# A transformer block on one core: where four of seven kept sums wait, when two columns of x are made, and two products in plain fp32

## The chip, the core and the metric

The kernel runs on one core of a Trainium2 chip. The core has five engines with instruction streams of their own: TensorE (PE, matrix products; its weight loads are shown as PEld), VectorE (DVE), ScalarE (ACT), GpSimd (POOL) and SyncE (SP). They meet at semaphores. SP's queue issues the loads, POOL's the transfers that add into their destination. The metric is the time of one launch on the device in microseconds (us), lower is better. The time before is 1423.77 us, the median of three runs (1421.55 to 1423.99).

## The reference

One decoder layer over 256 tokens of width 2048, in fp32: attention and a short gated convolution, merged by sigmoid gates; then a squared-ReLU MLP of width 8192, and a gated embedding. Cut to what matters here, the MLP and what follows it:

```python
h = rms_norm(r, g_mlp[i])
r = r + jnp.square(jax.nn.relu(h @ w_up[i])) @ w_down[i]
h = rms_norm(r, g_ple[i])
r = r + jax.nn.sigmoid(h @ w_ple_gate[i]) * (p[i] @ w_ple_proj[i])
```

## The kernel before

**Products.** A product in fp32 is made of three in fp32r: the operands are split into a high part (a copy on ACT, `high`) and a low part (a subtraction on DVE, `low`), and PE adds high·high, high·low and low·high. A product can also be left in plain fp32, without the split; PE then takes more time for it, and the kernel calls such pairs NATIVE (line 687): before, only the last pair, and of it only T1 and T3.

**The up/down stage** (lines 963 to 1066) runs over 72 units `g`: 64 columns of w_up, then 8 of w_down. A unit's column product (`cols`, ps_up or ps_dn) is followed on PE by the seven products P1 to P7 of one *pair* of the down product, which is done by a scheme of Strassen and Winograd: 7 products of 2x2 blocks in place of 8. A pair is (side, j); its blocks of w_down come as four loads into a `raw_s` tile (`load_pair`), and `make` forms B11, B22, B21 and the sums T1 to T4 from them; S1 to S4 are sums of the activations. T1 and T3 of three pairs in eight (ADDED, line 688) are not added by DVE: the blocks are loaded into a tile with the tag `t` (two rooms, `load_added`), and a DMA of POOL adds the other blocks to it (line 706). The seven products stay in PSUM banks from pair to pair.

**The two sides.** Side 0 and side 1 take the banks in turns. When a side ends, the seven sums go out (`store`): ACT evacuates a bank to a `part` tile, and a DMA of POOL adds it to a room in device memory. Side 0 comes back for good at pair (0, 20), in unit 51 to 52 (`resumed`): then its seven kept sums, loaded back in unit 46 (`fetch_kept`, RESUME), are copied into the banks (`resume`, on ACT for P1, P5, P2 and P4, on DVE for the others), each right behind the evacuation of the other side's sum from that bank. These steps stand in the list `filling` and are let in one by one between the work of `make` and of the next unit.

**Rooms and order.** `part`, the kept sums, x and many others come from one pool of 44 slots; a tile that finds no free slot waits until one is released, and the instruction that writes it waits with all that stands behind it on its engine. From unit 2 on every engine keeps the program's order (`inorder`), and so does SP's queue: a load that waits for a room holds those behind it.

**The end of the stage.** In units 69 to 71, x for the gate's products is entered from the finished columns of r (`enter_high` on ACT, `enter_low` on DVE): 8 and 9, then 10 to 12, then 13 and 14. In unit 71, p1 (P1 scaled, on ACT), d, e and f begin the four blocks c11, c12, c21 and c22 of the down product. PE goes on with `half_gate(0, 1)` over columns 8 to 15, and then transposes c11 and c21 (`turn`).

Of the kernel before, what the change touches and what calls it, by code (L numbers as in the profile page):

```python
# [8 lines left out]
F32 = mybir.dt.float32  # L9
# [9 lines left out]
P = 128  # L19
# [5 lines left out]
CW = 512  # L25
# [13 lines left out]
def hybrid_block_kernel(ctx: ExitStack, tc: tile.TileContext, ins: dict, out: bass.AP):  # L39
# [12 lines left out]
    wp = ctx.enter_context(tc.tile_pool(name="wp", bufs=N_PART))  # L52
# [5 lines left out]
    def slot(shape, dtype, name):  # L58
        return bp.tile(shape, dtype, tag="slot", name=name)
# [35 lines left out]
    def load(*args):  # L95
        dma = nc.sync.dma_start(*args)
        return tc.keep_in_program_order(dma) if ordered[0] or ordered_loads[0] else dma
# [37 lines left out]
    def high(hi, src):  # L135
        act(hi, src, AF.Copy)
# [417 lines left out]
    for c in range(4):  # L554
        gates = []
        for i in range(2):
            ps = rows(tiles("w_in", 24 + 16 * i + 4 * c), xT, f"g{i}_{c}", pops=2)
            g = [slot([P, CW], F32, f"g{i}_{c}_{t}") for t in range(NT)]
# [54 lines left out]
    N_GROUP, GROUP = 6, 4  # L613
    N_BOTH = N_GROUP * GROUP
    hP = {}
    uT, u_raw, wS, sums, wU, evac = {}, {}, {}, {}, {}, {}
# [4 lines left out]
    NU = len(units)  # L621
# [4 lines left out]
    items = []  # L626
# [14 lines left out]
    g = FIRST  # L641
# [32 lines left out]
    def half_tiles(name):  # L674
        return tuple(wp.tile([P, HALF], F32R, tag=t, name=f"{name}_{t}") for t in ("hi", "lo"))
# [9 lines left out]

    LAST = len(items) - 8
    NATIVE = {items[-1]}
    ADDED = {items[n] for n in range(GROUP, LAST) if (n - GROUP) % (2 * GROUP) in (0, 4, 6)} | set(items[LAST:])

    def pair_part(a, n, d):  # L690
        side, j = a
        n += 16 * (j // 8) + 8 * side
        k = 2 * (j % 8) + d
        return ins["w_down"][n:n + 4, :, k * P:(k + 1) * P].rearrange("n p m -> p n m")
# [3 lines left out]
    def load_pair(a):  # L698
# [3 lines left out]
        for i, block in enumerate(BLOCKS):  # L702
            if i != 2 or a not in ADDED:
                load(raw[:, i, :].rearrange("p (n m) -> p n m", n=4), pair_part(a, *block))
        if a in ADDED:
            nc.gpsimd.dma_start(wS[a]["t13"], raw[:, 0:2, :], accum_op=ALU.add)  # L706

    def load_added(a):

        wS[a] = {}  # L710
        if a in ADDED:
            t = wS[a]["t13"] = wp.tile([P, 2, CW], F32, tag="t", name="t13", bufs=2)
# [3 lines left out]
    def sum_u(j):  # L716

        a11, a12, a21, a22 = (u_raw[2 * j + k][:, t * P:(t + 1) * P] for t in range(2) for k in range(2))
        s = slot([P, 4, P], F32, "s_raw")
        dve.tensor_sub(s[:, 0, :], a21, a22)  # L720
        dve.tensor_sub(s[:, 2, :], s[:, 0, :], a11)
        dve.tensor_sub(s[:, 1, :], a11, a21)
        dve.tensor_add(s[:, 3, :], a12, s[:, 2, :])
        return s
# [13 lines left out]
    def make(a, xs, evacuate, work):  # L738


        w, j = wS[a], a[1]
        raw = w["raw"]
        flat, halves = "p a f -> p (a f)", "p (a f) -> p a f"
        fresh = None
        if 0 in xs:
            if j not in sums:
                fresh = sum_u(j)
                sums[j] = tuple(slot([P, 4, P], F32R, f"s_{i}") for i in range(2))
            sh, sl = sums[j]
            for i, name in enumerate(("S1", "S3", "S2", "S4")):  # L750
                w[name] = sh[:, i, :], sl[:, i, :]
            if a in NATIVE:
                w["S1"], w["S3"] = fresh[:, 0, :], fresh[:, 1, :]
                fresh, sh, sl = (t[:, 2:, :] for t in (fresh, sh, sl))
            hi, lo = half_tiles("b")
            keep(w, ("B11", "B22"), hi, lo)
            src = raw[:, 0:2, :].rearrange(flat)
            high(hi, src)
            evacuate()
            if fresh is not None:  # L760
                high(sh, fresh)
            low(lo, src, hi)
            if a in ADDED:
                t13 = w["t13"]
            else:
                t13 = raw[:, 0:3:2, :]
                dve.tensor_add(t13, raw[:, 0:2, :], raw[:, 2:3, :].to_broadcast([P, 2, CW]))
            w["raw13"] = t13
        if 2 in xs:
            b21 = w["B21"] = tuple(slot([P, CW], F32R, f"b21_{n}") for n in range(2))  # L770
            high(b21[0], raw[:, 3, :])
            evacuate()
            fill()
            dve.tensor_add(raw[:, 1, :], raw[:, 1, :], w["raw13"][:, 0, :])
            if 0 in xs:
                low(b21[1], raw[:, 3, :], b21[0])
                dve.tensor_add(raw[:, 3, :], raw[:, 1, :], raw[:, 3, :])
                raw24 = raw[:, 1:4:2, :]
            else:
                dve.tensor_add(raw[:, 2, :], raw[:, 1, :], raw[:, 3, :])  # L780
                low(b21[1], raw[:, 3, :], b21[0])
                raw24 = raw[:, 1:3, :]
                work()
        if 0 in xs:
            if fresh is not None:
                low(sl, fresh, sh)
            if 2 not in xs:
                work()
            if a in NATIVE:
                w["T1"], w["T3"] = w["raw13"][:, 0, :], w["raw13"][:, 1, :]  # L790
                fill()
            else:
                t13 = half_tiles("t13")
                keep(w, ("T1", "T3"), *t13)
                view = [t.rearrange(halves, a=2) for t in t13]
                high(view[0], w["raw13"])
                fill()
                low(view[1], w["raw13"], view[0])
        if 2 in xs:
            t24 = half_tiles("t24")  # L800
            keep(w, ("T2", "T4"), *t24)
            view = [t.rearrange(halves, a=2) for t in t24]
            high(view[0], raw24)
            fill()
            low(view[1], raw24, view[0])
# [6 lines left out]
    NAMES = ("P1", "P3", "P5", "P7", "P2", "P6", "P4")  # L812

    def products(a, x):
        j = a[1]
        for name, left, b, n0, n1 in PRODUCTS[x]:
            if a in first_of and a != resumed and n0 == 0:
                prod[name] = pp.tile([P, CW], F32, tag=f"b{int(name[1]) - 1}", name=name)
            if left[0] == "A":
                at = slice((int(left[1]) - 1) * P, int(left[1]) * P)  # L820
                k = 2 * j + int(left[2]) - 1
                xs = [uT[k][:, h, at] if k in uT else first_half(k)[:, h, :] for h in range(2)]
            else:
                xs = wS[a][left]
            if a in NATIVE and b in ("T1", "T3"):
                if n0 == 0:
                    mm(prod[name], xs, wS[a][b], start=False, skip_group_check=True, stop=a in last_of or a == items[-1])
                continue
            for n in range(n0, n1):
                mm(prod[name], xs[n == 2], wS[a][b][n == 1], start=a in first_of and a != resumed and n == 0, skip_group_check=a in items[resumed_at:], stop=(a in last_of or a == items[-1]) and n == 2)  # L830
# [12 lines left out]
    def scaled(dst, src, by, other, how=ALU.add):  # L843
        dve.scalar_tensor_tensor(dst, src, by, other, op0=ALU.mult, op1=how)
# [3 lines left out]
    resumed = [a for a in items if a in first_of][-1]  # L848
    resumed_at = items.index(resumed)

    def fetch_kept():
        kept = {}
        for name in NAMES:
            kept[name] = slot([P, CW], F32, "part_in")
            load(kept[name], parts[0, name])
        return kept

    def resume(name, st):
        prod[name] = pp.tile([P, CW], F32, tag=f"b{int(name[1]) - 1}", name=name)
# [26 lines left out]
    def fill(n=1):  # L886
        for _ in range(min(n + (n == 1 and len(filling) > 7), len(filling))):
            filling.pop(0)()
# [32 lines left out]
    def enter_high(n):  # L921
        hP[n] = slot([P, 2, S], F32R, "x")
        act(hP[n][:, 0, :], r[n // 2][:, n % 2, :], AF.Copy, scale=col(G_PLE + n))

    def enter_low(n):
        x = hP[n]
        dve.scalar_tensor_tensor(x[:, 1, :], r[n // 2][:, n % 2, :], col(G_PLE + n), x[:, 0, :].bitcast(F32), op0=ALU.mult, op1=ALU.subtract)
# [25 lines left out]
    RESUME, SUMS = 46, (56, 59)  # L953
# [9 lines left out]
    for g in range(NU):  # L963
        kind, i = units[g]
# [10 lines left out]
            if x == 0:  # L975
                load_added(a)
        if g == RESUME:
            kept = fetch_kept()
        if g in SUMS:
            sum_part(SUMS.index(g))  # L980
        for u in {NU - 8: (4, 5, 6, 7), NU - 4: (0, 1), NU - 3: (2, 3)}.get(g, ()):
# [6 lines left out]
        xs = hT if kind == "up" else {k: uT[16 * i[0] + k] for k in range(16)}  # L988
# [56 lines left out]
        if g == NU - 1:  # L1045
            p1 = [evacuated(prod["P1"], "p1", by) for by in (up0, up1)]
            d, e = (slot([P, CW], F32, n) for n in "de")
            scaled(d, prod["P5"], up0, p1[0], ALU.subtract)
            scaled(e, prod["P3"], up0, d)
            f = slot([P, CW], F32, "f")  # L1050
            scaled(f, prod["P7"], up1, p1[1])
        entering = {NU - 3: (8, 9), NU - 2: (10, 11, 12), NU - 1: (13, 14)}.get(g, ())
        for n in entering:
            enter_high(n)
            if n % 2 == 1:
# [198 lines left out]
```

## Time and profile before

| | |
|---|---|
| median of three timed runs | 1423.77 us |
| the profiled execution | 1418.83 us |
| its span | 1416.9 us |
| granted TensorE clock | 0.999 |
| ACT busy | 880.3 us (62%) |
| DVE busy | 1103.2 us (78%) |
| POOL busy | 202.3 us (14%) |
| HBM, read and written | 294.43 and 22.54 MB |

A row of a timeline shows the start and the length in us, the engine, line, operation, and what is written and read, with partitions x elements; a bracket gives the idle time of the engine just before it, and what ended that. "x3" means three instructions merged. Nearly every PE, ACT and DVE row has the line of a helper (90, 87, 101), so the tiles tell them apart. Buffer numbers are left out: P is any of the seven sums, t_hi the high part of T1/T3 or of T2/T4, t a tile of the two rooms. A row of the view of waits gives the time in all, the number of times and the longest. A row of the view of windows gives, for a stretch, its length, the busy time of PE, PEld, DVE, ACT and POOL, and then the granted clock, the share of the DMA engines and GB/s. In the view of DMA issues the last number is the time from issue to landing.

### The profile page before, as it was taken

The numbers are of one execution on the slowest core, as the hardware profiler recorded it, in microseconds if no ns is written. First come the engines' busy times: TensorE is split into PE (matmuls) and PEld (weight loads), VectorE is DVE, ScalarE is ACT, GpSimd is POOL, SyncE is SP. The second block draws the span as 40 slices with busy tenths as digits, with TensorE's granted clock in tenths as the row PEclk, the third lists the DMA queues.
The fourth block names the chain that finished last, engine by engine and source line by source line (L and its number), as shares of the span: only waits on it lengthen the run. The fifth ranks groups of instructions, "written<-read, shape, count | busy, mean of one in ns | idle before, by whom it ended". The sixth has DMA issues, their size and how long they took to land.

```text
span 1416.9 us, 19839 instructions
## 1 busy us (share of the span) xinstructions
PE 1406.4 (99%) x7023; PEld 1192.1 (84%) x7023; DVE 1103.2 (78%) x1676; ACT 880.3 (62%) x1433; POOL 202.3 (14%) x311
## 2 busy tenths in 40 slices
PE   9999999999999999999999999999999999999998
PEld 7888888888888888888888888888888878888888
DVE  7666666766555656665999999999998989888984
ACT  6765545554535444445777777778786767655752
POOL 0034464311120200000010100101010010110000
PEclk9999999999999999999999999999999999999999
DMA  9868787775666675663788888989899799998470
GB/s 290 305 218 261 221 245 231 234 224 198 219 202 213 210 266 191 211 223 95 225 279 248 266 244 238 276 257 256 259 233 318 236 237 271 272 284 268 154 255 23
DMA packets 220547, 331.39 MB, mean 234 GB/s; under 512 B 13600, under 2 KB 145184, under 8 KB 206368
## 3 DMA queue, kind: packets, MB, share of 16 engines
q1 hardware_dynamic: 201936, 287.08, 62.3%
q0 software_dynamic: 18368, 43.01, 13.2%
q8 instruction: 55, 0.90, 0.3%
q14 instruction: 44, 0.36, 0.1%
q10 hardware_dynamic: 144, 0.04, 0.0%
HBM read 294.43 MB, written 22.54 MB: 224 GB/s over the span
## 4 chain that ended last, share of the span: by engine, by line
PE 86%; DMA 5%; DVE 4%; issue 2%; ACT 2%; SPq 0%; POOL 0%; DVEq 0%; POOLq 0%; ACTq 0%
PE ps_up L90 20%; PE P L90 14%; PE ps_g L90 12%; PE ps_o L90 7%; PE ps_pg L90 6%; PE ps_y L90 6%; PE ps_q L90 3%; PE ps_cx L90 3%; PE ps_k L90 3%; PE ps_cb L90 3%; PE ps_cc L90 3%; PE ps_v L90 3%; DMA raw_s<-in_w_down_dram 2%; DVE w_lo L101 1%; DMA t<-in_w_down_dram 1%
## 5 line engine op out<-in xcount | busy, mean ns | idle before, releaser
L101 DVE TENSOR_TENSOR w_lo<-raw,w_hi 128x512 fp32r<-128x512 f32 (+1 forms) x524 | 467.9, 926 | 187.3 <-ACT w_hi L87 161.9
L87 ACT ACTIVATE w_hi<-raw 128x512 fp32r<-128x512 f32 (+1 forms) x524 | 407.0, 815 | 258.9 <-PE ps_g L90 63.1
L90 PE MATMUL ps_up<-x,w_hi 128*128 128x512 f32 x1024 | 253.4, 390 | 0.0
L90 PEld LDWEIGHTS ps_up<-x,w_hi 128*128 128x128 f32 x1024 | 192.0, 188 | 37.8 <-ACT up L87 0.6
L90 PE MATMUL ps_g<-w_hi,x 128*128 128x512 f32 x512 | 158.2, 389 | 0.0
L87 ACT ACTIVATE t_hi<-raw_s 128x1024 fp32r<-128x1024 f32 x88 | 93.5, 1062 | 94.3 <-DVE raw_s L101 94.2
L90 PEld LDWEIGHTS ps_up<-x,w_lo 128*128 128x128 f32 x1024 | 131.3, 191 | 5.0
L90 PE MATMUL ps_up<-x,w_lo 128*128 128x256 f32 x1024 | 132.8, 283 | 0.0
L90 PE MATMUL P<-t_hi,s 128*128 128x512 f32 x332 | 121.3, 392 | 2.6 <-ACT P L87 1.4
L90 PEld LDWEIGHTS ps_g<-w_hi,x 128*128 128x128 f32 x512 | 96.1, 188 | 19.9
L101 DVE TENSOR_TENSOR t_lo<-raw_s,t_hi 128x1024 fp32r<-128x1024 f32 x88 | 106.3, 1220 | 4.8 <-ACT t_hi L87 4.8
L101 DVE TENSOR_TENSOR raw_s<-raw_s 128x512 f32<-128x512 f32 (+1 forms) x120 | 100.1, 834 | 4.1
L90 PE MATMUL ps_g<-w_lo,x 128*128 128x512 f32 x256 | 99.6, 389 | 0.0
L706 POOL DMA_DIRECT2D t<-raw_s x24 | 20.5, 853 | 479.8 <-DVE b_lo L101 122.5
L90 PE MATMUL ps_y<-w_hi,x 128*128 128x512 f32 x256 | 79.4, 389 | 0.0
L90 PEld LDWEIGHTS P<-t_hi,s 128*128 128x128 f32 x332 | 62.6, 189 | 16.7 <-ACT P L87 2.5
L101 DVE TENSOR_TENSOR b_lo<-raw_s,b_hi 128x1024 fp32r<-128x1024 f32 x56 | 68.2, 1218 | 4.0 <-ACT b_hi L87 4.0
L90 PE MATMUL ps_pg<-x,w_hi 128*128 128x512 f32 (+1 forms) x272 | 67.9, 380 | 1.0 <-DVE x L101 1.0
L87 ACT ACTIVATE up<-ps_up 128x512 f32<-128x512 f32 x64 | 37.7, 590 | 45.3 <-PE ps_up L90 45.2
L90 PE MATMUL P<-t_lo,s 128*128 128x512 f32 x166 | 64.9, 391 | 0.0
L87 ACT ACTIVATE a<-a 128x256 f32<-128x256 f32 x128 | 53.2, 415 | 11.3 <-DVE a L101 9.5
L87 ACT ACTIVATE b_hi<-raw_s 128x1024 fp32r<-128x1024 f32 x56 | 58.8, 1050 | 0.0
(239 smaller groups left out, 2547.3 us busy)
## 6 DMA issues: line engine op xcount, KB each, us to landing
raw<-in_w_up_dram SPq DMA_DIRECT2D x64, 1024.0 KB, 7.3
raw<-in_w_in_dram SPq DMA_DIRECT2D x56, 1024.0 KB, 5.4
raw_s<-in_w_down_dram SPq DMA_DIRECT2D x200, 256.0 KB, 4.5
raw<-in_w_branch_dram SPq DMA_DIRECT2D x16, 1024.0 KB, 5.7
raw<-in_w_o_dram SPq DMA_DIRECT2D x16, 1024.0 KB, 4.9
raw_first<-in_w_qkv_dram SPq DMA_DIRECT2D x48, 256.0 KB, 6.4
raw<-in_w_qkv_dram SPq DMA_DIRECT2D x12, 1024.0 KB, 6.8
t<-in_w_down_dram SPq DMA_DIRECT2D x48, 256.0 KB, 5.9
```

What stands on the lines that cost most here:

```text
L87: return inorder(nc.scalar.activation(*args, **kw))
L90: return inorder(nc.tensor.matmul(*args, **kw))
L101: return lambda *args, **kw: inorder(getattr(nc.vector, name)(*args, **kw))
L706: nc.gpsimd.dma_start(wS[a]["t13"], raw[:, 0:2, :], accum_op=ALU.add)
```

## The change

Four things. The kept sums are fetched in three lots: P5, P7 and P2 in slots in unit 46; P1 and P3 in one `t` room in unit 47; P6 and P4 in one in unit 49. The pair that would have used that room, (0, 20), is no longer ADDED, so DVE adds its T1 and T3. Column 13 of x is entered in unit 70 with 10 to 12, and column 14 between p1, d and e in unit 71. And the last pair's T2 and T4 are left in plain fp32, as T1 and T3 were, with S2 and A22 unsplit.

```diff
-    ADDED = {items[n] for n in range(GROUP, LAST) if (n - GROUP) % (2 * GROUP) in (0, 4, 6)} | set(items[LAST:])
+    ADDED = {items[n] for n in range(GROUP, LAST) if (n - GROUP) % (2 * GROUP) in (0, 4, 6)} - {items[LAST - GROUP]} | set(items[LAST:])
...
             if a in NATIVE:
-                w["S1"], w["S3"] = fresh[:, 0, :], fresh[:, 1, :]
-                fresh, sh, sl = (t[:, 2:, :] for t in (fresh, sh, sl))
+                for i, name in enumerate(("S1", "S3", "S2")):
+                    w[name] = fresh[:, i, :]
+                w["A22"] = u_raw[2 * j + 1][:, P:]
+                fresh, sh, sl = (t[:, 3:, :] for t in (fresh, sh, sl))
...
-        if 2 in xs:
+        if 2 in xs and a in NATIVE:
+            w["T2"], w["T4"] = raw24[:, 0, :], raw24[:, 1, :]
+            fill()
+        elif 2 in xs:
             t24 = half_tiles("t24")
...
-            if left[0] == "A":
+            if left in wS[a]:
+                xs = wS[a][left]
+            else:
                 at = slice((int(left[1]) - 1) * P, int(left[1]) * P)
                 k = 2 * j + int(left[2]) - 1
                 xs = [uT[k][:, h, at] if k in uT else first_half(k)[:, h, :] for h in range(2)]
-            else:
-                xs = wS[a][left]
-            if a in NATIVE and b in ("T1", "T3"):
+            if a in NATIVE and b[0] == "T":
...
-    def fetch_kept():
-        kept = {}
-        for name in NAMES:
-            kept[name] = slot([P, CW], F32, "part_in")
+    kept = {}
+
+    def fetch_kept(names, pair=False):
+        if pair:
+            room = wp.tile([P, 2, CW], F32, tag="t", name="kept", bufs=2)
+        for i, name in enumerate(names):
+            kept[name] = room[:, i, :] if pair else slot([P, CW], F32, "kept")
             load(kept[name], parts[0, name])
-        return kept
...
         if g == RESUME:
-            kept = fetch_kept()
+            fetch_kept(NAMES[2:5])
+        if g == RESUME + 1:
+            fetch_kept(NAMES[:2], pair=True)
+        if g == RESUME + 3:
+            fetch_kept(NAMES[5:], pair=True)
...
             d, e = (slot([P, CW], F32, n) for n in "de")
+            enter_high(14)
             scaled(d, prod["P5"], up0, p1[0], ALU.subtract)
+            enter_low(14)
             scaled(e, prod["P3"], up0, d)
...
-        entering = {NU - 3: (8, 9), NU - 2: (10, 11, 12), NU - 1: (13, 14)}.get(g, ())
+        entering = {NU - 3: (8, 9), NU - 2: (10, 11, 12, 13)}.get(g, ())
```

`NAMES` is P1, P3, P5, P7, P2, P6, P4. Three places of the instruction streams show what moves.

ACT in unit 51 and 52, from the first evacuation of the ending side on. P1 to P4 are the banks, `part` the evacuated sums, part_in and kept the kept ones, t13_hi and t24_hi the high parts of T1/T3 and T2/T4. In brackets stands what an instruction waits for: PE, DVE, ACT itself, a DMA of SP (DMAHW) or of POOL (DMASW). Before:

```order
L87 ACTIVATE part_10677<-P1_9926 128x512 [waits PE_49]
L87 ACTIVATE P1_10680<-part_in_10061 128x512 [waits Activation_49]
L87 ACTIVATE t13_hi_10685<-t13_10385 128x1024 [waits DMAHW1_49,DMAHW0_49,DMASW0_49]
L87 ACTIVATE part_10688<-P3_9930 128x512 [waits DMASW4_49,Activation_49]
L87 ACTIVATE t24_hi_10694<-raw_s_10488 128x1024 [waits DVE_49]
L87 ACTIVATE part_10697<-P5_9934 128x512 [waits DMASW1_49]
L87 ACTIVATE P5_10700<-part_in_10065 128x512 [waits Activation_49]
L87 ACTIVATE w_hi_10745<-raw_10592 128x1024 [waits DMAHW6_49]
L87 ACTIVATE part_10748<-P7_9938 128x512 [waits DMASW5_49,DVE_49]
```

The same rows of the change:

```order
L87 ACTIVATE part_10673<-P1_9926 128x512 [waits PE_49]
L87 ACTIVATE P1_10676<-kept_10167 128x512 [waits Activation_49]
L87 ACTIVATE t13_hi_10681<-raw_s_10483 128x1024 [waits DMAHW3_49,DVE_49]
L87 ACTIVATE part_10684<-P3_9930 128x512 [waits PE_49]
L87 ACTIVATE t24_hi_10690<-raw_s_10483 128x1024 [waits DVE_49]
L87 ACTIVATE part_10693<-P5_9934 128x512 [waits PE_49]
L87 ACTIVATE P5_10696<-kept_10061 128x512 [waits Activation_49]
L87 ACTIVATE w_hi_10741<-raw_10587 128x1024 [waits DMAHW5_49]
L87 ACTIVATE part_10744<-P7_9938 128x512 [waits PE_49]
```

The order is the same; the evacuations of P3, P5 and P7 no longer wait for a DMA of POOL, and t13_hi reads what DVE added rather than a `t` room. Further down, P6's and P4's evacuations wait for one both before and after, now those of P1's and P3's `part`.

SP's queue in units 46 and 47 (a kept sum is a load from part_P; t is a load to a `t` room, raw a unit's weights, raw_s a pair's blocks). Before:

```order
L96 DMA part_in<-part_P_5543 128x512
L96 DMA part_in<-part_P_5544 128x512
L96 DMA part_in<-part_P_5545 128x512
L96 DMA part_in<-part_P_5546 128x512
L96 DMA part_in<-part_P_5547 128x512
L96 DMA part_in<-part_P_5548 128x512
L96 DMA part_in<-part_P_5549 128x512
L96 DMA raw<-in_w_up_dram 128x2048
L96 DMA raw_s<-in_w_down_dram 128x4x128 x4
L96 DMA t_10172<-in_w_down_dram 128x4x128 x2
L96 DMA raw<-in_w_up_dram 128x2048
```

The same stretch of the change:

```order
L96 DMA kept<-part_P_5545 128x512
L96 DMA kept<-part_P_5546 128x512
L96 DMA kept<-part_P_5547 128x512
L96 DMA raw<-in_w_up_dram 128x2048
L96 DMA raw_s<-in_w_down_dram 128x4x128 x4
L96 DMA t_10164<-in_w_down_dram 128x4x128 x2
L96 DMA kept<-part_P_5543 128x512
L96 DMA kept<-part_P_5544 128x512
L96 DMA raw<-in_w_up_dram 128x2048
```

Three loads stay ahead of unit 46's raw; P1 and P3 now stand ahead of unit 47's, and wait for a `t` room that the pair at work in that unit releases with its t13_lo on DVE.

DVE at the end of the stage, in unit 71: d, e and f, then x of columns 13 and 14, then the first blocks of the down product. Before:

```order
L101 SCALAR_TENSOR_TENSOR d_12432<-P5_10700,scales_5620,p1_12428 128x512 [waits PE_49,Activation_49]
L101 SCALAR_TENSOR_TENSOR e_12433<-P3_10691,scales_5620,d_12432 128x512 [waits DVE_49]
L101 SCALAR_TENSOR_TENSOR f_12436<-P7_10751,scales_5620,p1_12430 128x512 [waits PE_49,Activation_49]
L101 SCALAR_TENSOR_TENSOR x_12438<-r_6_11808,vec_72,x_12438 128x256 [waits PE_49,Activation_49]
L101 SCALAR_TENSOR_TENSOR x_12442<-r_7_11810,vec_72,x_12442 128x256 [waits Activation_49]
L101 SCALAR_TENSOR_TENSOR c11_12458<-P2_10762,scales_5620,p1_12428 128x512 [waits PE_49]
L101 SCALAR_TENSOR_TENSOR u3_12459<-P6_10771,scales_5620,f_12436 128x512 [waits DVE_49,PE_49]
L101 SCALAR_TENSOR_TENSOR c21_12461<-P4_10776,scales_5620,u3_12459 128x512 [waits DVE_49,PE_49]
```

The same of the change:

```order
L101 SCALAR_TENSOR_TENSOR d_12429<-P5_10696,scales_5620,p1_12425 128x512 [waits PE_49,Activation_49]
L101 SCALAR_TENSOR_TENSOR x_12431<-r_7_11806,vec_72,x_12431 128x256 [waits Activation_49]
L101 SCALAR_TENSOR_TENSOR e_12430<-P3_10687,scales_5620,d_12429 128x512 [waits DVE_49,PE_49]
L101 SCALAR_TENSOR_TENSOR f_12436<-P7_10747,scales_5620,p1_12427 128x512 [waits PE_49]
L101 SCALAR_TENSOR_TENSOR c11_12446<-P2_10758,scales_5620,p1_12425 128x512 [waits PE_49]
L101 SCALAR_TENSOR_TENSOR u3_12447<-P6_10767,scales_5620,f_12436 128x512 [waits DVE_49,PE_49]
L101 SCALAR_TENSOR_TENSOR c21_12449<-P4_10772,scales_5620,u3_12447 128x512 [waits DVE_49,PE_49]
```

x of column 13 has left this stretch for the unit before, and x of column 14 has moved from behind f to between d and e.

## The prediction, made before the change was run

> **What bounds the kernel now.** First the page's row of busy time, then the view of waits of PE from 1100 us to the end.
>
> ```profile
> PE 1406.4 (99%) x7023; PEld 1192.1 (84%) x7023; DVE 1103.2 (78%) x1676; ACT 880.3 (62%) x1433; POOL 202.3 (14%) x311
> ```
> ```profile
> PE P L90 <- ACT P L87: 1.4, 2, 0.7
> PE P L90 <- DVE P L101: 1.2, 1, 1.2
> PE tr L537 <- DVE c L101: 1.0, 1, 1.0
> PE ps_pg L90 <- DVE x L101: 1.0, 1, 1.0
> ```
>
> PE sets the time. These four rows are all its idle time after 1100 us, and the change edits exactly those two places: the resumed sums (two rows on P) and the end of the up/down stage (tr and ps_pg). To see what the first costs, a normal round is read from the chain, and the stalled one from PE's timeline.
>
> ```profile
> 1151.79 4.78 PE P L90 x21
> 1156.57 5.55 PE ps_up L90 x32
> ```
> ```profile
> 1136.25 0.40 PE L90 MATMUL P<-b_hi,x_first 128*128 128x512 f32 x1
> ...
> 1138.53 0.50 PE L90 MATMUL P<-t_hi,s 128*128 128x512 f32 x1 [0.74 <-ACT P L87]
> ...
> 1140.72 0.79 PE L90 MATMUL P<-t_hi,s 128*128 128x512 f32 x1 [1.21 <-DVE P L101]
> ...
> 1151.62 0.40 PE L90 MATMUL P<-b_hi,x_first 128*128 128x512 f32 x1
> ```
> ```profile
> 1125.00:1150.00 25.00, 22.42 (x103) 17.33 (x102) 18.32 (x24) 17.60 (x30) 5.97 (x7) 0.93 0.93 230
> 1300.00:1325.00 25.00, 22.96 (x134) 19.49 (x133) 23.54 (x39) 16.12 (x28) 0.00 (x0) 1.00 0.36 114
> ```
>
> A round is 4.78 + 5.55 = 10.33 us, a product 4.78 / 21 = 0.228. From one round's first product to the next this one takes 1151.62 − 1136.25 = 15.37: **5.04 us lost**. That is more than the idle time, since the granted clock of the stretch is 0.93: 0.07 × 25 = 1.75 us of PE work more.
>
> Why it waits stands on ACT and DVE:
>
> ```profile
> 1129.32 0.60 ACT L87 ACTIVATE part<-P 128x512 f32<-128x512 f32 x1 [0.17 <-PE P L90]
> ...
> 1137.25 0.60 ACT L87 ACTIVATE part<-P 128x512 f32<-128x512 f32 x1 [4.29 <-DMA part_P<-part]
> ...
> 1143.81 0.60 ACT L87 ACTIVATE P<-part_in 128x512 f32<-128x512 f32 x1
> ```
> ```profile
> 1143.67 0.69 DVE L101 COPY P<-part_in 128x512 f32<-128x512 f32 x1
> ```
> ```profile
> DMA to landing us min/median/max: 4.8/7.0/9.1
> ```
>
> The third evacuation (P5) sits 4.29 us until a store of a `part` tile has landed. The order rows name it: before, that evacuation waits on a software DMA (DMASW), after, on PE alone; P1's part leaves ACT at 1129.92 and a store takes 7.0 us, which is 1137. So a slot is missing, and the seven kept sums hold seven.
>
> **The change, part by part.** *Four slots freed.* P3, P5 and P7 lose their DMASW wait. Two remain, of P6 and P4, on the stores of P1 and P3. What is late next is DVE's chain for the same pair: it isn't accumulated any more, so DVE makes T1 and T3 itself. The round before is of that kind:
>
> ```profile
> 1118.11 1.22 DVE L101 TENSOR_TENSOR b_lo<-raw_s,b_hi 128x1024 fp32r<-128x1024 f32 x1
> ...
> 1128.37 1.22 DVE L101 TENSOR_TENSOR b_lo<-raw_s,b_hi 128x1024 fp32r<-128x1024 f32 x1
> ```
> ```profile
> 1122.67 1.06 ACT L87 ACTIVATE t_hi<-raw_s 128x1024 fp32r<-128x1024 f32 x1 [0.98 <-DVE raw_s L101]
> ```
>
> There t_hi of T2/T4 starts 4.56 after b_lo. With b_lo at 1128.37 it is at 1132.93 and ends at 1133.99, and P5's evacuation stands right behind it: 3.26 sooner than 1137.25. What follows on ACT and DVE runs back to back: DVE's copy of P6 ended at 1143.67 + 0.69 = 1144.36, 7.11 after P5's evacuation began, so now at 1141.1. PE would want P6, its sixth product group, at 1136.25 + 15 × 0.228 = 1139.67. Left to itself this leaves a wait of 1.4 at P6: 5.04 − 1.4 = 3.6 saved.
>
> *Loads moved.* Of seven loads in iteration 46 only three stay. Behind them an accumulation had landed late, and DVE stood still:
>
> ```profile
> t<-raw_s POOLq DMA_DIRECT2D x1, 512.0 KB, 10.3
> ```
> ```profile
> t<-raw_s POOLq DMA_DIRECT2D x3, 512.0 KB, 6.1
> ```
> ```profile
> 1088.30 0.69 DVE L101 TENSOR_TENSOR raw_s<-raw_s,t 128x512 f32<-128x512 f32 x1 [3.26 <-issue]
> ...
> 1090.84 1.22 DVE L101 TENSOR_TENSOR t_lo<-t,t_hi 128x1024 fp32r<-128x1024 f32 x1
> ```
> ```profile
> 1084.82 0.60 ACT L87 ACTIVATE up<-ps_up 128x512 f32<-128x512 f32 x1 [1.97 <-PE ps_up L90]
> ...
> 1088.24 1.06 ACT L87 ACTIVATE t_hi<-t 128x1024 fp32r<-128x1024 f32 x1 [1.79 <-DMA t<-raw_s]
> ```
>
> The first row is that one accumulation (issued 1078), the second the median of three. If it lands 1.4 us sooner (8.9), DVE is 1.4 us ahead from 1088 on, P6's copy ends at 1139.7, and the wait at P6 is gone. DVE's lead stays until then: in a round it has next to no idle time, and PE's rounds are as long as its own (1128.37 − 1118.11 = 10.26). The lead can't exceed 3.26, and ACT, which at 1084.82 waited for PE, caps it below that. A megabyte out of that stretch should bring the landing near the median, 6.1; I take a lead over 1.4 and so the whole **5.04**. Bounds: 10.3 again, 3.6 or less saved; near 6.1, 5.04.
>
> *SP's queue.* P1 and P3 wait for a `t` room that t_lo frees at 1090.84 + 1.22 = 1092.06, and the raw load of that iteration is queued behind them.
>
> ```profile
> 1088.89 0.78 SPq L96 DMA_DIRECT2D raw<-in_w_up_dram  x1
> ```
> ```profile
> raw<-in_w_up_dram SPq DMA_DIRECT2D x1, 1024.0 KB, 7.7
> ```
> ```profile
> 1102.51 1.99 ACT L87 ACTIVATE w_hi<-raw 128x1024 fp32r<-128x1024 f32 x2
> ```
>
> Two issues of 0.5 (estimate: 0.78 is the one seen) put it at 1093.1, landing 1100.8; ACT reads it at 1102.51. Cost nothing, with 1.7 to spare; if the lead comes, both move forward together. P6 and P4 at iteration 49 are alike, with one accumulation fewer in the way.
>
> *The end.* T2/T4's split goes, x13 moves a unit up, and x14 goes between d and e.
>
> ```profile
> 1299.26 1.06 ACT L87 ACTIVATE t_hi<-raw_s 128x1024 fp32r<-128x1024 f32 x1 [2.52 <-DVE raw_s L101]
> ...
> 1305.51 1.26 ACT L87 ACTIVATE p<-P,scales 128x512 f32<-128x512 f32 x2
> 1306.65 0.52 ACT L87 ACTIVATE x<-r,vec 128x256 fp32r<-128x256 f32 x1
> ```
> ```profile
> 1300.35 1.22 DVE L101 TENSOR_TENSOR t_lo<-raw_s,t_hi 128x1024 fp32r<-128x1024 f32 x1 [0.58 <-ACT t_hi L87]
> ...
> 1306.55 0.74 DVE L101 SCALAR_TENSOR_TENSOR d<-P,scales,p 128x512 f32<-128x512 f32 x1
> 1307.33 0.75 DVE L101 SCALAR_TENSOR_TENSOR e<-P,scales,d 128x512 f32<-128x512 f32 x1
> ...
> 1308.66 0.87 DVE L101 SCALAR_TENSOR_TENSOR x<-r,vec,x 128x256 fp32r<-128x256 f32 x2
> ...
> 1310.95 0.75 DVE L101 SCALAR_TENSOR_TENSOR c<-P,scales,u 128x512 f32<-128x512 f32 x1
> ```
> ```profile
> 1297.32 1.88 PE L90 MATMUL P<-t,s_raw 128*128 128x512 f32 x4
> ...
> 1304.82 0.86 PE L90 MATMUL P<-b,x 128*128 128x512 f32 x3
> ```
>
> DVE drops 1.22 and 0.58 of idle time, takes 0.44 for x13, and is free by 1305. But d needs p1, whose first half ACT ends at 1306.14 (half of 1.26 after 1305.51): d starts there, 0.4 sooner, not 1.4. Then x14's low half waits for its high half (ACT 1306.65 + 0.52 = 1307.17), and e follows 0.44 later, at 1307.6. From e to the last c took 3.62; without the two x (0.87) it takes 2.75 to 2.83 (they overlap a little), so c starts at 1310.4 instead of 1310.95: **0.5 saved** for the transposes that wait for it. Two plain products take 1.88 against 0.86 for one split one, both with their drain: 0.2 to 0.4 more for the pair. PE had 2.0 us of waits there to hide it; without that cover it would be lost. Ends: 0.4 lost; 2.0 − 0.3 = 1.7 saved.
>
> *Sum.* 5.04 + 0.5 = 5.5 from the profiled execution's 1418.83 gives 1413.3. The median of the timed runs is 1423.77, 4.9 above that execution; the same difference from it gives **1418.3**.
>
> **Rivals.** *The wait moves to P6.* No lead, and PE waits 1.4 there. The clock decides the price. The first windows row shows 0.93 after idle times of 0.74 and 1.21 within 3.1 us; the second shows 1.00 although the waits view has 2.0 us of idle time there. So 1.4 may or may not be followed by 1.75 of lost clock: 3.6 or 1.85 saved, with the end 4.1 or 2.35: 1419.7 to 1421.4.
> The Trainium skill ("TensorE: Matmul & The Clock Gate", Part 1) says the array falls to half rate after an idle window of about 3.4 us; by that this gap would cost 1.4 alone (1419.7). This trace disagrees in part: its clock fell after gaps that were all shorter.
>
> *The landing is the limit.* P6 and P4 still wait for the stores of P1 and P3, and a store can take 9.1. P3's part comes behind P1's (done at 1129.92), a resume of 0.60 and a t_hi of 1.06: it is done at 1132.2, or at 1130 with a lead of two. P4's resume then ends 9.1 + 1.2 (its evacuation and itself) later, at 1142.5 or 1140.3, and PE wants it at 1139.67 + 0.68 = 1140.35: up to 2.1 us of wait, on DVE's lead again. It is of the same kind if the timed runs hold less of this stall than the profiled one; together 1422 to 1424, no change.
>
> *The queue blocks: slower.* Iteration 47's raw load lands after 1102.51. All DVE and ACT work up to P5's evacuation then shifts by as much. It has 3.26 to give, so beyond a landing at 1105.8, 12.7 after issue, the kernel is slower by the rest; at 15, 1425.6 (2.3 more, less 0.5 at the end, with PE's clock low as now). Against it stand 7.7 and 10.3, the longest landing quoted.
>
> **How the numbers follow.** Forecast, with the end's two bounds 1417.0 to 1419.2, 0.56; wait at P6 0.22, half of it over the mark; no change 0.12; queue 0.10. Under 0.2% (2.85 us) a measurement can't tell it from no change, so faster 0.56 + 0.11 = 0.67, same 0.11 + 0.12 = 0.23, slower 0.10. The range leaves out the queue and the larger part of no change: up to 1422.4. Below, 1417.0 less the 1.0 by which the three timed runs scatter around their middle: 1416.0.
>
> **What would show it.** Right: no DMA named before a part evacuation of P5; the resumed round at 10.3 to 10.8; clock 1.00 around it; DVE's wait for the accumulation near 1085 under 1.9; one wait for c left at the end, x gone. Wrong: PE waiting for P6 or P4; ACT waiting for a raw load at iteration 48; rows of PE waiting in the rounds after the resumed one.

## The result, and the profile after

| | before | changed |
|---|---|---|
| median of the timed runs | 1422.66 us (6 runs, 1418.73 to 1423.99) | 1414.43 us (6 runs, 1413.93 to 1415.14) |
| ratio, 95% interval | | 0.9948 (0.9933 to 0.9963) |
| the profiled execution | 1418.83 us | 1414.29 us |
| its span | 1416.9 us | 1412.5 us |
| the resumed round | 15.37 us | 10.33 us |
| granted clock, 1125 to 1150 us | 0.93 | 1.00 |

The kernel is faster, and by more than was forecast: 1414.43 lies below the range (1416.0 to 1422.4). Two things stand out in the table. The profiled executions differ by only 4.5 us and the timed medians by 8.2; and the runs of the kernel before spread over 5.3 us, those of the changed one over 1.2.

The first view is again the row of busy time, then the waits of PE from 1100 us on, then two stretches of the view of windows.

```profile
PE 1405.7 (100%) x7021; PEld 1191.3 (84%) x7021; DVE 1104.6 (78%) x1676; ACT 879.5 (62%) x1432; POOL 201.5 (14%) x310
```
```profile
PE tr L537 <- DVE c L101: 1.1, 1, 1.1
PE ps_dn L90 <- ACT dn L87: 0.4, 1, 0.4
```
```profile
1125.00:1150.00 25.00, 25.00 (x133) 21.54 (x132) 22.82 (x28) 21.28 (x34) 5.98 (x7) 1.00 1.04 255
1300.00:1325.00 25.00, 23.82 (x133) 19.57 (x133) 21.59 (x37) 15.31 (x27) 0.00 (x0) 1.00 0.31 101
```

Both rows on P are gone, and so is ps_pg <- x. One wait for c is left, and one of 0.4 on ps_dn that this profile of before did not show; a later profile of the kernel before shows two such waits, 0.9 us in all, so it need not come from the change. In the resumed stretch PE is busy all 25 us at full clock. The same place in the timelines of PE, ACT and DVE:

```profile
1136.93 0.40 PE L90 MATMUL P<-b_hi,x_first 128*128 128x512 f32 x1
...
1147.26 0.40 PE L90 MATMUL P<-b_hi,x_first 128*128 128x512 f32 x1
```
```profile
1130.33 0.58 ACT L87 ACTIVATE part<-P 128x512 f32<-128x512 f32 x1
...
1132.39 0.58 ACT L87 ACTIVATE part<-P 128x512 f32<-128x512 f32 x1
```
```profile
1126.86 1.22 DVE L101 TENSOR_TENSOR b_lo<-raw_s,b_hi 128x1024 fp32r<-128x1024 f32 x1
...
1138.79 0.69 DVE L101 COPY P<-kept 128x512 f32<-128x512 f32 x1
```

From one round's first product to the next are 10.33 us, an undisturbed round. P5's evacuation (the ACT row of 1132.39) has no bracket: it waits for nothing. P6's copy, the last one on DVE, ends at 1138.79 + 0.69 = 1139.48; PE wants it at 1136.93 + 15 × 0.228 = 1140.35, so 0.9 us are to spare.

Upstream, in units 46 and 47, the accumulation that had landed late, DVE's instruction that had waited 3.26 us for it, SP's queue and ACT's use of the load that now stands behind the kept sums:

```profile
t<-raw_s POOLq DMA_DIRECT2D x1, 512.0 KB, 7.0
```
```profile
1085.52 1.22 DVE L101 TENSOR_TENSOR b_lo<-raw_s,b_hi 128x1024 fp32r<-128x1024 f32 x1
1086.77 0.69 DVE L101 TENSOR_TENSOR raw_s<-raw_s,t 128x512 f32<-128x512 f32 x1
```
```profile
1090.56 0.81 SPq L96 DMA_DIRECT2D kept<-part_P  x2
1091.42 0.43 SPq L96 DMA_DIRECT2D raw<-in_w_up_dram  x1
```
```profile
raw<-in_w_up_dram SPq DMA_DIRECT2D x1, 1024.0 KB, 8.0
```
```profile
1100.99 1.99 ACT L87 ACTIVATE w_hi<-raw 128x1024 fp32r<-128x1024 f32 x2
```

It lands in 7.0 us instead of 10.3, and DVE's instruction on t has no wait in front. The two kept sums are issued at 1090.56, the raw load right behind at 1091.42; it lands at 1099.4, and ACT begins on it at 1100.99 without a bracket.

The end of the stage, on PE and then on DVE:

```profile
1300.89 0.86 PE L90 MATMUL P<-b,x 128*128 128x512 f32 x3
1301.59 1.02 PE L90 MATMUL P<-raw_s,s_raw 128*128 128x512 f32 x2
1302.44 1.02 PE L90 MATMUL P<-raw_s,a 128*128 128x512 f32 x2
1302.90 1.95 PE L90 MATMUL ps_pg<-x,w_hi 128*128 128x512 f32 x6
...
1307.31 0.87 PE L537 MATMUL tr<-ident,c 128*128 128x128 f32 x6 [1.07 <-DVE c L101]
...
1314.41 0.60 PE L537 MATMUL tr<-ident,c 128*128 128x128 f32 x4
```
```profile
1302.30 0.75 DVE L101 SCALAR_TENSOR_TENSOR d<-P,scales,p 128x512 f32<-128x512 f32 x1 [2.26 <-ACT p L87]
...
1306.50 0.75 DVE L101 SCALAR_TENSOR_TENSOR c<-P,scales,u 128x512 f32<-128x512 f32 x1
```
```profile
1318.86 0.60 PE L537 MATMUL tr<-ident,c 128*128 128x128 f32 x4
```

The last row is of before, which closes the same stretch there. In what follows **the end** means PE's time from the first product behind the last column (P<-b,x) to that second group of transposes: 1318.86 − 1304.82 = 14.04 before, 1314.41 − 1300.89 = 13.52 now, 0.52 less. d waits 2.26 us for p1 on ACT, as the prediction had it.

### The profile page after: what moved, and what is told of

Same layout as the page of the kernel before. It is cut to its first block, busy times and chain, and to the rows that moved or that the text cites. A ratio compares the mean times of both kernels' runs of the same rounds, so it can differ in the third digit from the quotient of the medians.

```text
span 1412.5 us, 19831 instructions
## 1 busy us (share of the span) xinstructions
PE 1405.7 (100%) x7021; PEld 1191.3 (84%) x7021; DVE 1104.6 (78%) x1676; ACT 879.5 (62%) x1432; POOL 201.5 (14%) x310
## 4 chain that ended last, share of the span: by engine, by line
PE 98%; DVE 1%; DMA 1%; ACT 0%; issue 0%; SPq 0%; DVEq 0%; ACTq 0%
PE ps_up L90 25%; PE P L90 18%; PE ps_g L90 12%; PE ps_o L90 7%; PE ps_pg L90 6%; PE ps_y L90 6%; PE ps_k L90 3%; PE ps_q L90 3%; PE ps_cx L90 3%; PE ps_cb L90 3%; PE ps_cc L90 3%; PE ps_v L90 3%; PE ps_dn L90 2%; PE ps_proj L90 1%; DMA t<-in_w_down_dram 1%; PE ps_s L90 0%
```

## The experiments

All eleven with their main numbers. "Round" is the resumed round on PE, from first product to first product. "Before" is the median of the kernel before in the runs of the same chip.

| kernel | us: median (range, runs) | before | round, us | end, us |
|---|---|---|---|---|
| kernel before, again | 1422.14 (1420.33 to 1423.60, 11) | 1421.69 | 16.33 | 14.07 |
| end only | 1421.36 (1419.38 to 1423.75, 11) | 1421.69 | 16.92 | 13.51 |
| kept sums only | 1416.28 (1414.39 to 1419.97, 6) | 1421.69 | 10.48 | 14.01 |
| loads again in unit 46 | 1416.12 (1414.55 to 1418.37, 5) | 1421.69 | 11.80 | 13.52 |
| changed, again | 1415.01 (1413.83 to 1415.51, 5) | 1421.14 | 10.32 | 13.52 |
| half of the rooms | 1416.80 (1414.95 to 1421.94, 10) | 1421.14 | 12.02 | 13.49 |
| pair not accumulated, alone | 1420.63 (1419.45 to 1425.39, 10) | 1421.14 | 16.57 | 14.02 |
| p1 early | 1413.56 (1413.10 to 1415.16, 5) | 1421.14 | 10.33 | 12.63 |
| changed, T2 and T4 split | 1416.36 (1) | 1421.74 | 10.33 | 15.84 |
| changed, x as before | 1415.37 (1) | 1421.74 | 10.32 | 13.72 |
| p1 early, e late | 1413.78 (1412.02 to 1414.89, 6) | 1421.74 | 10.33 | 12.48 |

### Where the runs of before spread

The kernel before, unchanged:

> The kernel before, unchanged, for the spread of its runs. Stall theory: the 4 to 5 us by which most timed runs of before stand above its profiled one (1418.83) are lost at the resumed round, where the granted clock falls further than the 0.93 that the profile shows. Then the runs lie between 1418 and 1424, and each run above 1421 has a mean granted clock of 0.998 or less (4 us of 1420 are 0.003). Rival (it is lost elsewhere, in waits for DMAs that differ from run to run): the runs scatter as much, at a clock of 0.999 to 1.000 in all.

Its round took 1153.56 − 1137.23 = 16.33 us. The view of windows of this run, around the end of the wait:

```profile
1142.00:1146.00 4.00, 1.68 (x6) 0.96 (x5) 1.04 (x3) 2.11 (x5) 1.70 (x2) 0.94 1.11 237
1146.00:1149.00 3.00, 3.00 (x8) 1.99 (x8) 2.45 (x3) 1.45 (x4) 0.00 (x0) 0.52 1.05 344
1149.00:1153.00 4.00, 4.00 (x26) 3.53 (x25) 3.97 (x5) 3.01 (x4) 0.00 (x0) 1.00 0.60 118
```

The 0.93 of a 25 us stretch is not a mild slowing. It is 3.41 us at half the clock (1145.49 to 1148.90 in this run's trace), 1.7 us lost, and then full clock. In the run whose profile the prediction read, the same thing lay earlier:

```profile
1137.00:1141.00 4.00, 2.05 (x8) 1.09 (x7) 1.03 (x2) 3.72 (x6) 1.62 (x2) 0.93 1.03 254
1141.00:1144.00 3.00, 2.87 (x6) 1.38 (x6) 2.60 (x4) 2.97 (x8) 1.65 (x3) 0.52 1.03 147
```

There the half clock (1140.47 to 1143.88) ran while PE waited for the late sums anyway. P4's sum, the last one, was in its bank at 1143.81 + 0.60 = 1144.41, so slow products ahead of it cost little. In the run above P4's sum came at 1145.47, just before the slow part.

Over all 66 timed runs of the kernel before that came with the experiments, the median is 1421.47 (1419.30 to 1426.68). By mean granted clock, 11 runs at 0.995 or 0.996 have a mean of 1423.85, 24 at 0.997 or 0.998 one of 1421.64, and 31 at 0.999 or 1.000 one of 1420.84. So the slower runs are mostly those with more of the low clock; the groups lie 3 us apart in a spread of 7. The bound that the expectation set for single runs did not hold, since runs up to 1422.3 show 1.000. The 15 runs at 1.000 alone lie between 1419.30 and 1422.32, and one spell of 3.41 us at half is 0.0012 of the mean, so some 3 us of the spread come without such a spell, in part as the rival had it. What spreads the runs there was not found, and the mean clock of a run without a trace doesn't say where in it the clock fell.

### The parts alone

```diff
 kept sums only: before, with the edits of ADDED, fetch_kept and its calls
 end only:       before, with the edits of make, products, p1 to f and entering
```

> The changed kernel with the end of the stage as before: only the kept sums' rooms and the pair that is no longer accumulated. Stall theory: nearly the whole gain, 1414.5 to 1415.5 in the median, and all runs within 1.5 us of each other, since the place that scattered is gone; the resumed round is 10.3 us. Rival: the median is 1416.5 to 1418 (5 us saved from any run of before) and the scatter stays at 4 to 5 us.

> Only the end of the stage changed (T2 and T4 of the last pair plain, x of columns 13 and 14 sooner). Stall theory: the median within 1 us of before, 0.5 lower by the working of the prediction, with before's scatter of 4 to 5 us, and the stalled round of 15 us is there. Rival (the scatter comes from the waits at the end, 2 us of PE idle time in four us): the scatter is gone, and the median is 3 us or more lower.

The kept sums bring most of it (5.4 us by the medians, where the changed kernel saves 6.1 to 6.7), and the round is 10.48. The end alone can't be told from before by the clock (ratio 1.0001, 0.9993 to 1.0010), yet its 13.51 on PE is the 13.52 of the changed kernel. Two expectations missed. The median of the kept sums alone, 1416.28, is above the 1414.5 to 1415.5 of the stall theory; and its runs still spread, over 5.6 us, as the rival had it. The slowest run (1419.97) is the one at the lowest clock (0.998). That kernel keeps the two waits of 1.0 us at the end; whether the clock fell behind them in that run is not shown, since the run that was traced has no low clock there.

In the kernel with the end alone the round was 16.92, with two spells of low clock back to back:

```profile
1138.00:1142.00 4.00, 2.07 (x8) 1.05 (x6) 0.68 (x2) 3.37 (x5) 1.27 (x2) 1.00 1.05 272
1142.00:1146.00 4.00, 3.10 (x7) 1.55 (x8) 3.30 (x5) 3.97 (x10) 2.65 (x4) 0.56 1.13 150
1146.00:1150.00 4.00, 4.00 (x11) 3.15 (x12) 3.17 (x4) 2.45 (x4) 0.35 (x1) 0.58 0.96 275
```

### Rooms or pair

```diff
-    ADDED = {... in (0, 4, 6)} | set(items[LAST:])
+    ADDED = {... in (0, 4, 6)} - {items[LAST - GROUP]} | set(items[LAST:])
```

> The kernel before with one edit alone: pair (0, 20) is no longer accumulated, so DVE adds its T1 and T3; the seven kept sums stay in slots from unit 46 on. Slot theory: the stalled round stays, 15 to 17 us, and the time is that of before within 1 us. Rival: it takes 3 us or more off, since the third evacuation no longer waits so long.

Without the rooms the round is 16.57, and the time is that of before (0.9999, 0.9988 to 1.0011). P5's evacuation still waits for a store, though DVE is not late (its b_lo stands 1126.72 − (1136.50 − 10.33) = 0.55 us behind the start of its round):

```profile
1135.33 0.60 ACT L87 ACTIVATE part<-P 128x512 f32<-128x512 f32 x1 [2.12 <-DMA part_P<-part]
```

Taking the pair out of the accumulation is only the means to a free `t` room.

Half of the rooms, in the changed kernel:

```diff
-            fetch_kept(NAMES[2:5])
+            fetch_kept(NAMES[2:])
...
-        if g == RESUME + 3:
-            fetch_kept(NAMES[5:], pair=True)
```

> The changed kernel with half of the rooms: only P1 and P3 wait in a t room, P6 and P4 in slots from unit 46 on as before. If the slots are what costs, the wait for a store comes back two sums later: P7's evacuation waits for P1's store (about 1 us on ACT), P2's, P6's and P4's for P3's, P5's and P7's; PE waits at P6 and P4, 1 to 3 us slower than the changed kernel, 2.5 to 5 faster than before. If the freed slots don't matter (the pair that is no longer accumulated does it alone): as the changed kernel, within 0.5 us.

ACT's rows of this kernel, P7's evacuation and P4's, PE's one wait on P, and DVE's wait for the accumulation in unit 47:

```profile
1137.39 0.60 ACT L87 ACTIVATE part<-P 128x512 f32<-128x512 f32 x1 [0.65 <-DMA part_P<-part]
...
1141.64 0.60 ACT L87 ACTIVATE part<-P 128x512 f32<-128x512 f32 x1 [0.29 <-DMA part_P<-part]
```
```profile
1142.56 0.47 PE L90 MATMUL P<-t_hi,s 128*128 128x512 f32 x1 [0.92 <-DVE P L101]
```
```profile
1088.96 0.69 DVE L101 TENSOR_TENSOR raw_s<-raw_s,t 128x512 f32<-128x512 f32 x1 [1.84 <-issue]
```

Waits for a store come back at P7 and P4 (the expectation had P2 and P6 as well), shorter than before and from P7 on rather than P5, and PE waits for P6. The round is 12.02, 1.7 longer than with all rooms; the median is 1.8 above the changed kernel's on that chip, with runs that spread over 7 us. This run doesn't price the slots by themselves, though: its five loads in unit 46 also delay the accumulation (it lands after 8.8 us), and DVE waits for it, as in the next experiment, where nearly the same is lost with all slots free. The two that separate them are the pair alone (16.57) and the next one (11.80): both have seven loads of kept sums in unit 46, with accumulations that land after 9.6 and 9.2 us, and up to that round they differ in the slots and in four later loads. So the slots are worth 4.8 us of the round (16.57 − 11.80), with the low clock that goes with the longer wait.

### DVE's lead

```diff
         if g == RESUME:
             fetch_kept(NAMES[2:5])
+            for name in NAMES[:2] + NAMES[5:]:
+                load(slot([P, CW], F32, "again"), parts[0, name])
```

> The changed kernel, with P1, P3, P6 and P4 loaded once more in unit 46 into free slots that nothing reads, so that the traffic there is that of before. DVE's lead theory: the accumulation behind them lands late again (about 10 us after issue), DVE waits some 3 us for it in unit 47, its lead of 2.2 us over PE is gone, and PE waits 1.3 us for P6 in the resumed round; 1 to 3.5 us slower than the changed kernel. Rival (the free slots alone save the round): no wait of PE there, within 0.5 us of the changed kernel.

The accumulation in that run's view of DMA issues, DVE's wait for it, PE's wait in the round, and DVE's copy of P6:

```profile
t<-raw_s POOLq DMA_DIRECT2D x1, 512.0 KB, 9.2
```
```profile
1089.48 0.69 DVE L101 TENSOR_TENSOR raw_s<-raw_s,t 128x512 f32<-128x512 f32 x1 [1.67 <-issue]
```
```profile
1142.35 0.47 PE L90 MATMUL P<-t_hi,s 128*128 128x512 f32 x1 [1.09 <-ACT P L87]
```
```profile
1141.51 0.69 DVE L101 COPY P<-kept 128x512 f32<-128x512 f32 x1
```

With the megabyte back ahead of it the accumulation lands at 9.2 instead of 7.0, DVE waits, and the round is 11.80: 1.5 us longer. PE's wait is put down to ACT, not to DVE, but at the sum that was meant: by its start, 1137.68 + 15 × 0.228 = 1141.1, the product is the first of P6's group, and DVE's copy of P6 ended at 1142.20, right before it. The clock stayed at 1.00. So free slots alone are not enough for an undisturbed round; the loads had to leave unit 46 too. By the timed runs this can't be told: the kernel saves 5.6 us against before on its chip, the changed one 6.1 on another, with intervals of the ratio that overlap (0.9952 to 0.9976 and 0.9942 to 0.9965). The expected 1 to 3.5 us are shown by the trace alone.

### The changed kernel again

> The changed kernel, unchanged, for more runs of both kernels on one chip. If the step that failed is the base (three timed runs with a median of 1423.77, where 34 runs of the kernel before have one of 1422.0) and not the saving, the saving is 5 to 6.5 us here, and the changed kernel's median 1415 to 1416.5. If the saving itself was put too low, it is 7 or more again and the median 1414.5 or less, with all runs within 1.5 us.

The saving is 6.1 us by the medians, ratio 0.9954 (0.9942 to 0.9965), and the median 1415.01. The first reading (the base) holds for the most part; the eleven runs of the changed kernel together have a median of 1414.81, 6.7 below the 66 of before.

### The end, in parts, and made shorter

```diff
 T2 and T4 split: changed, without the edits of make and products
 x as before:     changed, without enter_high(14) and enter_low(14) among p1 to f, and with
                  {NU - 3: (8, 9), NU - 2: (10, 11, 12), NU - 1: (13, 14)}
```

> The changed kernel with T2 and T4 of the last pair split as before; x of columns 13 and 14 stays sooner. Measured on PE from the first product behind the last column to the second group of transposes: 14.04 us before, 13.52 changed. If moving x won the 0.5: 13.5 to 13.6, since d waits for p1 and DVE, 1.8 us later, is still free before it. If dropping the split won it: 14.0.

> The changed kernel with x of columns 13 and 14 made in unit 71 behind f as before; T2 and T4 plain. Over the same stretch: if moving x won the 0.5, 13.7 to 14.0 (d 0.3 sooner, but both x ahead of c11 again, and PE waits for x as before, 0.7 to 1.0 us). If dropping the split won it: 13.5.

The first missed by far. With the split kept and x of column 13 moved into unit 70, DVE has more to do there than before, and d starts 2.70 us behind the last column's end instead of 1.41. PE, with x at hand, runs into the transposes:

```profile
1306.49 0.44 PE L537 MATMUL tr<-ident,c 128*128 128x128 f32 x2 [1.52 <-DVE c L101]
1308.00 1.54 PE L537 MATMUL tr<-ident,c 128*128 128x128 f32 x6 [1.07 <-DVE c L101]
```
```profile
1304.00:1308.00 4.00, 1.41 (x10) 0.96 (x8) 3.90 (x8) 0.00 (x0) 0.00 (x0) 0.98 0.23 92
1308.00:1311.00 3.00, 3.00 (x10) 2.66 (x11) 2.36 (x6) 1.76 (x3) 0.00 (x0) 0.50 0.00 0
```

2.6 us of waits close together, then half the clock: 15.84 us for the end, of which about 1.7 is the clock; the other 14.1 are what before took, as the second of the expected cases (14.0) had it. The low clock was not expected. Dropping the split without moving x gives 13.72, 0.3 of the 0.52. So the plain products pay, and the earlier x pays only on top of them, as far as one traced run of each kernel shows.

The 2.26 us that d waits for p1 can go: P1, P3, P5 and P7 are complete before the last column starts.

```diff
+        if g == NU - 1:
+            p1 = [evacuated(prod["P1"], "p1", by) for by in (up0, up1)]
+            ... (d, x of column 14, e and f, as in the changed kernel)
         fill(carried)
         if staged[g]:
             make(...)
         take()
-        if g == NU - 1:
-            ... (the same lines)
```

> The changed kernel with p1, d, e, f and x of column 14 ahead of the last column's evacuation: the four sums that they read are done 6 us before it, and DVE stood 2.26 us waiting for p1. c21 then starts some 2.5 us sooner, and the 1.07 us that PE waits for it are gone: 1.0 us faster than the changed kernel by the trace from the last column to the transposes, no more than 0.1% by the clock. Rival: c21 waits for P4 on PE instead, or x of columns 13 and 14 comes late for the gate's products, and nothing is won.

The wait for c is gone, the end takes 12.63 us (0.89 less than changed), and a new wait stands there, for x of column 15:

```profile
1307.73 0.38 PE L90 MATMUL ps_pg<-x,w_lo 128*128 128x256 f32 x1 [0.49 <-ACT x L87]
```

By the clock it is 1413.56 against 1415.01 on the same chip, with ranges that overlap. Then e was moved too:

```diff
-            scaled(e, prod["P3"], up0, d)
...
     enter_high(15)
     square(7)
+    scaled(e, prod["P3"], up0, d)
```

> The kernel with p1 early, and e moved from ahead of f to behind the high part of x of column 15, where DVE stands 0.58 us. The 0.49 us that PE waited for that x are gone: 12.1 to 12.2 us over the stretch, after 12.63 with p1 early alone; 1413.1 to 1413.6 by the clock, which can't tell it from that kernel. Rival: something else stands there, and nothing is won.

This missed: 12.48, and the same wait, now 0.53. x of column 15 is 0.6 us sooner, but PE arrives there sooner by as much, since its transposes fall differently. Both kernels are the fastest of the study (ratios to before 0.9946, 0.9934 to 0.9958, and 0.9939, 0.9922 to 0.9955); that they beat the changed kernel is shown by the trace of the end, not by the clock.

## Why the prediction missed its range

**Bounds.** Right: the two edited places were PE's only idle time in that profile from 1100 us on, and both went as forecast.

**Four slots freed.** Right, and tested: no DMA stands ahead of P5's evacuation, and without the rooms (pair not accumulated, alone) the wait and the long round are there. For P6 and P4, which still wait for stores by the order, no wait shows.

**Loads moved, and DVE's lead.** Right. DVE's b_lo stood 1128.37 − (1136.25 − 10.33) = 2.45 us behind the start of its round before, and 1126.86 − (1136.93 − 10.32) = 0.25 now: a lead of 2.2, where 1.4 were needed. (In the repetition of before it stood 1.17 behind, so the lead differs from run to run.) Without it (loads again in unit 46) the round was 1.5 longer, where 1.4 were forecast; and the clock, which the rival left open for such a single wait, stayed at 1.00. The wait at P6 is thus a real rival with the right price; the landing decided against it.

**SP's queue.** Right: forecast 1093.1 for the raw load's issue, 1100.8 for its landing and 1.7 us to spare; it came to 1091.42, 1099.4 and 1.6.

**The end.** Forecast 0.5, measured 0.52. That two plain products cost 0.2 to 0.4 more on PE is right too. The stretch that is called the end, before and now:

```profile
1304.82:1318.86 14.04, 12.00 (x66) 9.69 (x65) 13.19 (x24) 7.42 (x13) 0.00 (x0) 1.00 0.24 78
```
```profile
1300.89:1314.41 13.52, 12.34 (x65) 9.42 (x64) 11.14 (x19) 6.51 (x11) 0.00 (x0) 1.00 0.29 103
```

PE is busy 0.34 us longer, and idle 0.86 less (14.04 − 12.00 = 2.04, 13.52 − 12.34 = 1.18). The starts of the rows hide that: the gate's first product is shown from 1302.90 on, while the last plain one runs until 1302.44 + 1.02 = 1303.46. The prediction credited part of the gain to DVE being free early and part to x; the split's removal is the part without which the other wins nothing.

**The sum** is where it failed. The saving of 5.5 us gave 1413.3 from the profiled execution, and the changed kernel's own profiled execution took 1414.29. (PE's rounds start 0.7 us later in that run than in before's, 1126.61 against 1136.25 − 10.33 = 1125.92, and the wait of 0.4 on ps_dn is in that run and not in the profile of before.) The step that failed is the next one: "The median of the timed runs is 1423.77, 4.9 above that execution; the same difference from it gives 1418.3." The forecast stands 3.87 above the measured median, and these divide so:
- 2.3 is the base: three runs with a median of 1423.77 stood for a kernel whose 66 runs have one of 1421.47 and spread over 7 us. The "1.0 by which the three timed runs scatter", which set the lower end of the range, was far too little for that.
- 1.2 is the saving (1421.47 − 1414.81 = 6.66, not 5.5). The term that was mis-sized is the **5.04** of the resumed round. It was read from the lightest case: in the four profiles with the stall (before, its repetition, the end only, the pair alone) it cost 15.37, 16.33, 16.92 and 16.57, less 10.33 each: 5.04, 6.00, 6.59 and 6.24, in the mean 5.97. In each, P4's sum stands in its bank 8.2 to 8.3 us after the round's start, where a free round uses it after 18 × 0.228 = 4.1. So 4.1 us are fixed by the late store, and 0.9 to 2.5 more come with the low clock, by where its 3.4 us fall, or 6.8 in the kernel with the end alone. The prediction took the clock of one run as the price.
- 0.4 is the difference between the six first runs of the changed kernel and all eleven.

The difference between profile and timed runs was thus no constant to be carried over. One profiled execution is one run of a kernel that spreads: the one of before (1418.83) lies below all 66 later runs, 2.6 us under their median, and the profile of its repetition (1422.14) lies 0.7 above it. For the changed kernel, whose stall is gone, it is 0.5 (1414.81 against 1414.29). That the low clock adds to the spread of before's runs is borne out by the clock of 66 runs and by four traces; it doesn't account for all of it.

## What to carry to other kernels

A stall on TensorE costs its idle time and, in some runs, one or two spells of half clock behind it. Where the timed runs of a kernel spread, a base of three runs and the price of a stall in one profile are both terms with an error, and the distance between profile and median is nothing to carry over to the changed kernel. The removal of the stall may take off part of the spread: the changed kernel's 11 runs lie within 1.7 us, but with the kept sums alone they still spread over 5.6. When a pool runs short, count for each waiting tile whose release it needs; and when a transfer is moved out of a crowded stretch, look for the engine that had stood still behind it, since its lead may decide the place far downstream.

## What the hardware showed that was not expected

The granted clock has two values in these traces, full and half, and half lasts 3.41 us or twice that: 3.41 in the profile of before and in its repetition, and 6.83 in the kernel with the end alone. The changes of the clock lie on a grid of that length through the whole run: in before it goes to full at 3.83 us and to half at 1140.47, 333 times 3.413 later. And it needs no idle stretch of that length. Two windows of that grid in the profile of before, the one ahead of the drop and the one with the two waits at the end of the stage:

```profile
1137.06:1140.47 3.41, 1.71 (x7) 0.75 (x5) 0.50 (x1) 3.19 (x5) 1.09 (x2) 1.00 1.01 262
1307.72:1311.14 3.42, 2.00 (x13) 1.29 (x11) 3.32 (x7) 0.36 (x1) 0.00 (x0) 1.00 0.19 78
```

PE was busy 1.71 us in the first, half of the window, and the clock fell at its end; it was busy 2.00 us in the second, and the clock stayed. The same holds in all 13 traces: the clock fell after the windows of the grid with 1.71 (before), 1.14 (its repetition), 1.42 (end only), 1.35 (pair alone) and 0.99 us (T2 and T4 split) of PE work, and after no window between 8 and 1405 us with 2.00 or more. So the line lies between 1.71 and 2.00 of 3.41 here, as far as five drops show, and where a wait falls on the grid decides whether it costs clock: a stretch cut anywhere else, such as 4 us around a wait, doesn't tell. It went back to full after windows with 3.15 us or more; in the kernel with the end alone, 2.58 us left it at half for one more.

The Trainium skill ("TensorE: Matmul & The Clock Gate", Part 1) speaks of a free-running window of about 3.4 us and of half rate after one idle window. The length agrees with these runs; that the window must be idle does not.
